# A row-sum of reciprocals: loads and chains of two rows in place of four, seven whole rows in place of sixteen, six single rows at the end

## The chip, the core and the metric

The kernel runs on one core of a Trainium2 chip; the other cores are idle. The time is the device time in microseconds of one execution. A single-core run is judged fast when it lies within 1.5% of the fastest of the same kernel.

The engines are named as the profile names them: DVE is VectorE, ACT is ScalarE, POOL is GpSimd, SP issues the loads.

## The reference

```python
x: (32, 512, 1024) float32, positive           # 67.1 MB
return np.sum(1.0 / x, axis=-1)                # 16384 sums
```

Each of the 128 partitions gets 128 rows of 1024 numbers. A "row" below always means one such row in each of the 128 partitions: 512 KB.

## The kernel before

A row is summed in one of two ways.

- By product ("chain"). For the two halves a and b of a row, 1/a + 1/b = (a + b) / (ab). POOL forms the products ab (512 numbers for 1024), ACT takes Ln and then Exp(-Ln) of them, which is 1/(ab), and DVE multiplies the row by it and sums. The work on ACT is halved, and POOL and DVE are brought in.
- Whole. ACT takes Ln and Exp(-Ln) of all 1024 numbers and sums in the same pass. POOL and DVE do nothing.

`GROUPS` lists (rows by product, whole rows, engine of the product), and each group is one load and one chain:

```python
    GROUPS = (
        [(1, 1, GP), (2, 0, GP)]
        + [(3, 1, GP), (4, 0, GP)] * 14
        + [(3, 1, GP), (2, 0, GP), (2, 0, GP)]
        + [(1, 0, GP), (1, 0, GP), (1, 0, GP), (1, 0, DV)]
    )
    xpool = ... bufs=8        # loaded rows: 8 x 4 rows x 4 KB per partition
    ppool = ... bufs=4        # products
    rpool = ... bufs=2, PSUM  # 1/(ab)
    # ... cut ...
    for np_, ns, eng in GROUPS:
        n = np_ + ns
        xt = xpool.tile([P, n, D], f32, tag="xt")
        nc.sync.dma_start(out=xt, in_=x_v[:, c0 : c0 + n, :])
        pr = ppool.tile([P, np_, H], f32, tag="pr")
        eng.tensor_tensor(out=pr, in0=xt[:, :np_, :H], in1=xt[:, :np_, H:], op=mult)
        for j in range(np_, n):
            # ... whole rows: ACT Ln, ACT Exp with accum_out ...
        nc.scalar.activation(out=pr, in_=pr, func=Ln, scale=S)
        rc = rpool.tile([P, np_, H], f32, tag="rc")
        nc.scalar.activation(out=rc, in_=pr, func=Exp, scale=-1.0)
        for j in range(np_):
            # ... DVE: row * rc, summed into sums[:, c0 + j] ...
        c0 += n
    nc.sync.dma_start(out=out_v, in_=sums)
```

The build schedules the instructions: within an engine their order need not be the order written.

Of the kernel before, what the change touches and what calls it, by code (L numbers as in the profile page):

```python
# [1 line left out]

# [5 lines left out]


@with_exitstack  # L10
def kernel(
    ctx: ExitStack,
    tc: tile.TileContext,
    x: bass.AP,
    out: bass.AP,
):







    nc = tc.nc
    f32 = mybir.dt.float32
    P = 128
    D = 1024
    H = D // 2
    F = 128

    S = float(2**17)


    GP, DV = nc.gpsimd, nc.vector
    GROUPS = (
        [(1, 1, GP), (2, 0, GP)]
        + [(3, 1, GP), (4, 0, GP)] * 14
        + [(3, 1, GP), (2, 0, GP), (2, 0, GP)]
        + [(1, 0, GP), (1, 0, GP), (1, 0, GP), (1, 0, DV)]
    )  # L40

    Ln = mybir.ActivationFunctionType.Ln
    Exp = mybir.ActivationFunctionType.Exp
    mult = mybir.AluOpType.mult
    add = mybir.AluOpType.add

    x_v = x.flatten_outer_dims().rearrange("(p f) d -> p f d", p=P)
    out_v = out.flatten().rearrange("(p f) -> p f", p=P)

    act_sets = list(get_activation_tables(nc.m.arch).keys())  # L50
    nc.scalar.add_instruction(  # L51
        mybir.InstLoadActFuncSet(
            name=nc.get_next_instruction_name(),
            act_func_set_id=act_sets.index("natural_log_exp_and_others"),
            ins=[],
            outs=[],
        )
    )

    xpool = ctx.enter_context(tc.tile_pool(name="xpool", bufs=8))  # L60
    ppool = ctx.enter_context(tc.tile_pool(name="ppool", bufs=4))
    opool = ctx.enter_context(tc.tile_pool(name="opool", bufs=1))
    rpool = ctx.enter_context(
        tc.tile_pool(name="rpool", bufs=2, space=bass.MemoryType.PSUM)
    )

    sums = opool.tile([P, F], f32)

    c0 = 0
# [7 lines that stand above are left out]
            nc.scalar.activation(out=xt[:, j, :], in_=xt[:, j, :], func=Ln)  # L77
            nc.scalar.activation(  # L78
                out=xt[:, j, :],
                in_=xt[:, j, :],  # L80
                func=Exp,
                scale=-1.0,
                accum_out=sums[:, c0 + j : c0 + j + 1],
# [5 lines that stand above are left out]
            row = xt[:, j, :].rearrange("p (h e) -> p h e", h=2)  # L89
            nc.vector.tensor_tensor_reduce(  # L90
                out=row,
                in0=row,
                in1=rc[:, j, :].unsqueeze(1).to_broadcast([P, 2, H]),
                scale=S,
                scalar=0.0,
                op0=mult,
                op1=add,
                accum_out=sums[:, c0 + j : c0 + j + 1],
            )
        c0 += n  # L100
    assert c0 == F, c0

    nc.sync.dma_start(out=out_v, in_=sums)


# [1 line left out]
_INS = ['x']  # L107
_OUTS = [((32, 512), 'float32')]


# [23 lines left out]
```

## Time and profile before

| | before |
|---|---|
| time, first three runs | 179.79 us (179.39 to 180.21) |
| span of the profiled run (itself 180.0 us) | 178.2 us |
| the stream in the middle | 425 to 432 GB/s, DMA share 1.00 to 1.01 |
| ACT, DVE, POOL in the middle | 90%, 84%, 82% |
| last load landed | 162.7 us |
| from last landing to the end ("lag" below) | 15.5 us |

The table of stages of the kernel before; the columns are the stretch, its length, the busy time of each engine with its instructions, the granted clock, the DMA share (the mean busy share of the 16 DMA engines) and the GB/s:

```profile
core 0: us, DVE busy (x) ACT busy (x) POOL busy (x), PEclk, DMA share, GB/s
20.00:40.00 20.00, 13.10 (x23) 14.55 (x12) 13.90 (x5) 1.00 1.01 426
60.00:80.00 20.00, 16.76 (x31) 17.92 (x17) 16.41 (x5) 1.00 1.00 425
100.00:120.00 20.00, 16.75 (x29) 17.91 (x15) 16.41 (x5) 1.00 1.01 432
...
160.00:165.00 5.00, 4.64 (x9) 4.77 (x6) 4.23 (x4) 1.00 0.19 79
165.00:170.00 5.00, 5.00 (x9) 2.96 (x5) 0.00 (x0) 1.00 0.00 0
```

Read it from two ends. In the middle the DMA engines are full and no compute engine is: the load stream sets the pace. After 162.7 us nothing is loaded any more, and from 165 us DVE alone is full. These are the two terms of the time: the stream, and what is still to be done when it ends.

The stream runs near the most that can be had. The Trainium skill gives the fabric's ceiling as 435 GB/s ("DMA: Bandwidth & Descriptors", Specifications); the 425 to 432 GB/s here are 98 to 99% of it.

The trace also records when each load lands, as one mark by each of 16 DMA engines. A load counts as landed at its last mark. (To set these records against the span I took POOL's first product to start 0.06 us after the first landing.) In the middle a 2 MB load lands every 4.89 us: 1.22 us per row.

POOL at the end, from the timeline of the kernel before; the columns are start, duration, engine, line, operation, and the idle time before it:

```profile
137.70 4.54 POOL L75 TENSOR_TENSOR pr<-xt 128x2048 f32<-128x2048 f32 x1 [1.46 <-DMA xt<-in_x_dram]
142.60 3.45 POOL L75 TENSOR_TENSOR pr<-xt 128x1536 f32<-128x1536 f32 x1 [0.36 <-DMA xt<-in_x_dram]
147.50 4.54 POOL L75 TENSOR_TENSOR pr<-xt 128x2048 f32<-128x2048 f32 x1 [1.45 <-DMA xt<-in_x_dram]
152.38 11.91 POOL L75 TENSOR_TENSOR pr<-xt 128x1536 f32<-128x1536 f32 x6 [0.35 <-DMA xt<-in_x_dram]
```

POOL waits for every load until 152.38, then does six products back to back. DVE's reductions, which stand 1.14 us apart when nothing holds them up, run without a gap from 161.03 to the last row's product, which its timeline shows:

```profile
172.45 0.68 DVE L75 TENSOR_TENSOR pr<-xt 128x512 f32<-128x512 f32 x1
```

(The chain of waits, next, counts it from 172.53, when the reduction before it is done.) The last row is DVE's own from the product on, and the chain of waits of the kernel before ends with it:

```profile
172.53 0.61 DVE pr L75
173.14 0.02 issue
173.16 0.64 ACT pr L85
173.80 0.02 issue
173.82 0.61 ACT rc L87
174.44 0.02 issue
174.46 1.22 DVE xt L90
```

Product, Ln, Exp and reduction of the last row, 3.2 us one after the other, and another 2.5 us for the store.

### The profile page before, as it was taken

Reading aid. Unit: us, or ns where it says so; the run is one execution under the profiler, and the core shown is the slowest. Engines: PE = TensorE matmul, PEld = TensorE weight load, DVE = VectorE, ACT = ScalarE, POOL = GpSimd, SP = SyncE. Lnnn points to the kernel's source line nnn. Section 1 sums busy time; section 2 is a strip of 40 time slices with the busy share of each in tenths; the row PEclk is TensorE's granted clock in tenths of the full one; section 3 lists DMA queues with packets and bytes.
Section 4 is the critical chain, followed back from the end, with each engine's and each line's share of the span. In section 5 each row is a group of like instructions: output and inputs, shape, how many; then the busy total and the mean of one; then the engine's idle time right before and its main releaser. Section 6 shows DMA issues by size and latency. Waiting matters only on the chain. (4 is left out here: it accounts for less than half of the span.)

```text
span 178.2 us, 617 instructions
## 1 busy us (share of the span) xinstructions
DVE 131.3 (74%) x225; ACT 142.9 (80%) x123; POOL 127.4 (71%) x40
## 2 busy tenths in 40 slices
DVE  0043629749697987979797979879797979799982
ACT  2757399396998979797979989797979799899531
POOL 0446946959789696969697896969696978998000
DMA  5999899999999999999999999999999999991000
GB/s 202 445 416 430 349 423 438 412 416 430 449 416 416 450 423 416 434 439 419 416 449 427 416 430 445 419 416 449 427 416 421 452 416 414 409 365 66 0 0 15
DMA packets 5477, 67.22 MB, mean 377 GB/s; under 512 B 608, under 2 KB 736, under 8 KB 1248
## 3 DMA queue, kind: packets, MB, share of 16 engines
q1 hardware_dynamic: 5472, 67.18, 89.8%
q14 instruction: 5, 0.04, 0.1%
HBM read 67.11 MB, written 0.07 MB: 377 GB/s over the span
## 5 line engine op out<-in xcount | busy, mean ns | idle before, releaser
L90 DVE CUSTOM_DVE_ANT_1 xt<-xt,rc 128x1024 f32<-128x1024 f32 x112 | 130.4, 1218 | 44.4 <-POOL pr L75 18.8
L75 POOL TENSOR_TENSOR pr<-xt 128x1536 f32<-128x1536 f32 (+3 forms) x36 | 127.2, 3540 | 36.6 <-DMA xt<-in_x_dram 36.6
L85 ACT ACTIVATE pr<-pr 128x1536 f32<-128x1536 f32 (+3 forms) x37 | 54.9, 1486 | 22.8 <-POOL pr L75 20.6
L87 ACT ACTIVATE rc<-pr 128x1536 f32<-128x1536 f32 (+3 forms) x37 | 54.3, 1467 | 3.6 <-DVE sums L90 2.6
L77 ACT ACTIVATE xt<-xt 128x1024 f32<-128x1024 f32 x16 | 16.7, 1042 | 3.9 <-DMA xt<-in_x_dram 3.9
L78 ACT ACTIVATE xt<-xt 128x1024 f32<-128x1024 f32 x16 | 16.9, 1057 | 0.5
L90 DVE DVE_READ_ACCUMULATOR2_ANT sums<- 128x1 f32 x112 | 9.2, 82 | 0.0
L78 ACT ACTIVATION_READ_ACCUMULATOR xt<-xt 128x1 f32 x16 | 3.0, 186 | 0.0
L51 ACT ACT_TABLE_LOAD x1 | 1.3, 1283 | 0.7 <-PEq L118 0.7
L75 DVE TENSOR_TENSOR pr<-xt 128x512 f32<-128x512 f32 x1 | 0.7, 684 | 0.0
L118 POOL MEMSET const-float32-0.0<- 128x1 f32 x1 | 0.1, 98 | 0.2 <-issue 0.2
L118 POOL MEMSET const-bfloat16-1.0<- 128x1 bf16 x1 | 0.1, 101 | 0.0
L118 POOL MEMSET const-uint8-127<- 128x1 uint8 x1 | 0.1, 101 | 0.0
L118 POOL MEMSET const-float32-1.0<- 128x1 f32 x1 | 0.1, 98 | 0.0
## 6 DMA issues: line engine op xcount, KB each, us to landing
xt<-in_x_dram SPq DMA_DIRECT2D x29, 2048.0 KB, 26.7
xt<-in_x_dram SPq DMA_DIRECT2D x4, 1024.0 KB, 14.6
xt<-in_x_dram SPq DMA_DIRECT2D x4, 512.0 KB, 12.8
out_dram<-sums SPq DMA_DIRECT2D x1, 64.0 KB, 1.5
```

Of the source, the lines that this page charges most:

```text
L51: nc.scalar.add_instruction(mybir.InstLoadActFuncSet(name=nc.get_next_instruction_name(), act_func_set_id=act_sets.index("natural_log_exp_ ...
L75: eng.tensor_tensor(out=pr, in0=xt[:, :np_, :H], in1=xt[:, :np_, H:], op=mult)
L77: nc.scalar.activation(out=xt[:, j, :], in_=xt[:, j, :], func=Ln)
L78: nc.scalar.activation(out=xt[:, j, :], in_=xt[:, j, :], func=Exp, scale=-1.0, accum_out=sums[:, c0 + j : c0 + j + 1],)
L85: nc.scalar.activation(out=pr, in_=pr, func=Ln, scale=S)
L87: nc.scalar.activation(out=rc, in_=pr, func=Exp, scale=-1.0)
L90: nc.vector.tensor_tensor_reduce(out=row, in0=row, in1=rc[:, j, :].unsqueeze(1).to_broadcast([P, 2, H]), scale=S, scalar=0.0, op0=mult, op ...
L118: nc = _bacc.Bacc("TRN2", target_bir_lowering=False, num_devices=1)
```

## The change

Its intent: loads and chains of two rows let each engine start sooner and leave less behind when the stream ends; fewer whole rows relieve ACT, the busiest compute engine. The buffered bytes stay the same.

```diff
     GROUPS = (
-        [(1, 1, GP), (2, 0, GP)]
-        + [(3, 1, GP), (4, 0, GP)] * 14
-        + [(3, 1, GP), (2, 0, GP), (2, 0, GP)]
-        + [(1, 0, GP), (1, 0, GP), (1, 0, GP), (1, 0, DV)]
+        ([(2, 0, GP)] * 4 + [(1, 1, GP)] + [(2, 0, GP)] * 3) * 7
+        + [(2, 0, GP)] * 5
+        + [(1, 0, GP)] * 4 + [(1, 0, GP), (1, 0, DV)]
     )
...
-    xpool = ctx.enter_context(tc.tile_pool(name="xpool", bufs=8))
+    xpool = ctx.enter_context(tc.tile_pool(name="xpool", bufs=16))
```

## The prediction

> **What bounds the kernel now.** The load stream. The table of stages shows a DMA share of 1.00 to 1.01 and 425 to 432 GB/s in every 20 us stage from 20 to 140 us. The Trainium skill ("DMA: Bandwidth & Descriptors", Specifications) gives 435 GB/s as the fabric ceiling, so this is about 98% of it and cannot be sped up. In the same stages ACT is 90% busy, DVE 84%, POOL 82%: none is full, and the groups table puts all of POOL's 36.6 us of waiting on loads. Successive 2 MB landings in the trace are 4.89 us apart, 1.22 us per row.
>
> The second term is the tail. Loads stop at about 162 us, the span is 178.2. The timeline shows POOL working six products back to back until 164.3, then VectorE alone reducing its backlog of ten rows gaplessly at 1.14 us each until 172.5, then the last row's serial chain (0.68 + 0.63 + 0.60 + 1.22 us) and the store. The chain of waits contains only this end.
>
> **What changes.** All loads shrink from 2 MB to 1 MB (67 loads instead of 37); buffered bytes are unchanged (16 x 2 rows for 8 x 4), so the queue should stay full. Nine rows move from ScalarE alone to the three-engine path.
>
> *Loads, cost.* Packets become 8 KB: the packet records show 611 to 615 ns for 16 KB, 309 to 314 for 8 KB, 159 for 4 KB, i.e. some 9 ns fixed per packet. The same page ("Why small descriptors are slow") names a fixed cost per packet; the trace agrees. Two rows should take 2.47 to 2.495 us (seen between 1 MB landings at start and end), against 2.446. Over some 58 pairs: +1.3 to +2.8 us, plus about 0.1 for two more single-row loads. All on the critical path.
>
> *Engines, per 16 rows (now 19.8 us of loads).* POOL: 7 x 2.37 + 1.28 = 17.9 us. ACT: 7 x 2.07 + 1.22 + 2.15 = 17.9. DVE: 15 x 1.14 = 17.1. All below 19.8, so the middle stays bound by loads, with POOL's margin per pair only about 0.1 us. Fewer whole rows therefore buy nothing.
>
> *Tail, gain.* The lag behind the loads shrinks. Now the last three-row and two-row groups leave VectorE ten rows behind when POOL ends. After: the last pair lands some 7.5 us before the last load; then POOL 2.4, ACT 2.1, VectorE 2.3 + 5 single rows x 1.14, product to reduction 3.2, store 2.5. This is bound by VectorE: the end falls about 10.6 us after the last landing instead of about 15.4: some 4.5 us won.
>
> Net: about -2 to -3 us of 179.8. A small recurrence over these measured durations, which reproduces the span before to 0.2 us, gives 174.8 to 177.3 us of span.
>
> **Predicted: 177.2 us (175.3 to 179.2).** Faster by over 2%: 0.26; within 2%: 0.70; slower: 0.04.
>
> **What would show each step.** Loads: 8 KB packets at 309 to 314 ns; landings of pairs about 2.48 us apart; loads ending 1.5 to 3 us later, near 164. Middle: DMA share still 1.00, POOL about 90% busy and still waiting on loads. Tail: VectorE reduces gaplessly to the last row, but its last product begins near 169 to 170 instead of 172.5.
>
> **What would make it wrong.** POOL's 0.1 us margin vanishes (more waits per group), making the middle POOL-bound and the tail longer. DMA stalls: one near 16 to 19 us holds some engines about 2 us now; another count of these moves the result by as much. Two-deep PSUM with two-row tiles could stall ScalarE behind VectorE. If 8 KB packets cost nothing extra in a long stream, the gain exceeds 2%.

The "small recurrence" named there goes through the groups in order. A product starts when its load has landed and POOL is free; Ln when the product is done and ACT is free; Exp also waits until one of the two PSUM tiles is free; the reductions start when Exp is done and DVE is free. Every duration is one read from the trace before. The experiments' expectations use it too.

## The result, and the profile after

| | before | after |
|---|---|---|
| median time | 179.63 us (4 runs, 179.39 to 180.21) | 177.09 us (4 runs, 176.94 to 177.36) |
| ratio | | 0.9856, 95% interval 0.9828 to 0.9883 |
| span of the profiled run | 178.2 us | 174.9 us |
| landings, middle | 4.89 us per four rows | 2.485 us per two rows |
| last load landed | 162.7 us | 163.9 us |
| lag from there to the end | 15.5 us | 11.1 us |

A ratio is the mean time of one kernel's fast runs over that of the other's of the same rounds, so it is not quite the ratio of the medians. The change gains 1.4%, within the 2% that count here as the same. The two profiles differ by 3.3 us and the medians by only 2.5: about 0.4 us of that is the profiled run of before, one of its slower ones (180.0 us), and 0.3 us lies outside the spans (the time exceeds the span by 1.8 us before and by 2.1 after).

The table of stages of the changed kernel:

```profile
20.00:40.00 20.00, 19.18 (x33) 18.27 (x21) 17.92 (x9) 1.00 1.01 422
60.00:80.00 20.00, 17.92 (x31) 17.63 (x20) 17.89 (x9) 1.00 1.02 423
100.00:120.00 20.00, 16.97 (x31) 16.68 (x19) 16.94 (x9) 1.00 1.01 420
...
160.00:165.00 5.00, 4.87 (x9) 4.09 (x7) 4.89 (x4) 1.00 0.40 158
165.00:170.00 5.00, 4.70 (x9) 2.79 (x6) 0.00 (x0) 1.00 0.00 0
```

The DMA engines are still full, but move 420 to 424 GB/s in place of 425 to 432. POOL and DVE are 85 to 90% busy in these stretches from 60 us on, instead of 82% and 84%. The stream still ends near the same time (158 GB/s in the stretch from 160 to 165), and now less is left to do. Two lines of the changed kernel's DVE timeline, and then the end of its chain of waits:

```profile
167.87 1.22 DVE L89 CUSTOM_DVE_ANT_1 xt<-xt,rc 128x1024 f32<-128x1024 f32 x1
169.01 0.69 DVE L74 TENSOR_TENSOR pr<-xt 128x512 f32<-128x512 f32 x1
```

```profile
169.09 0.62 DVE pr L74
...
169.73 0.64 ACT pr L84
...
170.39 0.61 ACT rc L86
...
171.02 1.22 DVE xt L89
```

The last row's product begins at 169.01 in place of 172.45, straight after the reduction before it; DVE has no gap from 161.01 on. The last row's serial chain is as long as it was.

One thing was not as supposed. SP's own waits, of the kernel before and then of the changed kernel (total us, times, longest):

```profile
SPq L73 <- DVE sums L90: 137.5, 29, 7.6
```

```profile
SPq L72 <- DMA xt<-in_x_dram: 123.1, 59, 3.1
```

and the pages' lists of issues, with the KB of one and the median us to landing, in the same order:

```profile
xt<-in_x_dram SPq DMA_DIRECT2D x29, 2048.0 KB, 26.7
```

```profile
xt<-in_x_dram SPq DMA_DIRECT2D x61, 1024.0 KB, 19.8
```

Before, SP waits for DVE to free a buffer. After, it waits for earlier loads to land, and a load lands 19.8 us after it was issued: eight periods of 2.485 us. So eight loads are in flight, not the 12 or 13 that 16 buffers would leave room for (a pair is in work for 7.1 us from its landing to its last reduction, three periods). In both traces the loads carry eight different semaphores (counters that a landing raises and that an engine can wait on), taken in turn, and the issuing instructions of the changed kernel's trace show what holds the others back. The first eight loads are issued from 0.74 to 4.50 us without a wait. From the ninth on, the program itself makes SP wait for the semaphore of the load eight before: the first load lands at 5.54 and the ninth is issued at 5.55, the second at 8.35 and the tenth at 8.36. The limit is thus the built program's own; these runs show none of the chip's.

### The profile page after: what moved, and what is told of

Read it like the earlier page. It is cut to its first block, busy times and chain, and to the rows that moved or that the text cites. A ratio compares the mean times of both kernels' runs of the same rounds, so it can differ in the third digit from the quotient of the medians.

```text
span 174.9 us, 826 instructions
## 1 busy us (share of the span) xinstructions
DVE 143.5 (82%) x243; ACT 141.0 (81%) x156; POOL 142.7 (82%) x70
## 5 line engine op out<-in xcount | busy, mean ns | idle before, releaser
L89 DVE CUSTOM_DVE_ANT_1 xt<-xt,rc 128x1024 f32<-128x1024 f32 x121 | 142.5, 1219 | 28.7 <-ACT rc L86 14.2
L74 POOL TENSOR_TENSOR pr<-xt 128x1024 f32<-128x1024 f32 (+1 forms) x66 | 142.5, 2164 | 21.9 <-DMA xt<-in_x_dram 14.8
L84 ACT ACTIVATE pr<-pr 128x1024 f32<-128x1024 f32 (+1 forms) x67 | 64.8, 969 | 25.7 <-POOL pr L74 23.5
L86 ACT ACTIVATE rc<-pr 128x1024 f32<-128x1024 f32 (+1 forms) x67 | 63.1, 942 | 3.5 <-DVE sums L89 1.8
L89 DVE DVE_READ_ACCUMULATOR2_ANT sums<- 128x1 f32 x121 | 10.0, 83 | 0.0
L76 ACT ACTIVATE xt<-xt 128x1024 f32<-128x1024 f32 x7 | 7.3, 1040 | 0.0
L77 ACT ACTIVATE xt<-xt 128x1024 f32<-128x1024 f32 x7 | 7.3, 1040 | 0.0
L77 ACT ACTIVATION_READ_ACCUMULATOR xt<-xt 128x1 f32 x7 | 1.3, 186 | 0.0
## 6 DMA issues: line engine op xcount, KB each, us to landing
xt<-in_x_dram SPq DMA_DIRECT2D x61, 1024.0 KB, 19.8
```

What stands on the lines that cost most here:

```text
L76: nc.scalar.activation(out=xt[:, j, :], in_=xt[:, j, :], func=Ln)
L77: nc.scalar.activation(out=xt[:, j, :], in_=xt[:, j, :], func=Exp, scale=-1.0, accum_out=sums[:, c0 + j : c0 + j + 1],)
L89: nc.vector.tensor_tensor_reduce(out=row, in0=row, in1=rc[:, j, :].unsqueeze(1).to_broadcast([P, 2, H]), scale=S, scalar=0.0, op0=mult, op ...
```

## The experiments

The theory: (1) the middle is bound by the stream, so the mix of rows does not matter; (2) smaller packets make the stream about 2 us longer; (3) the finer end shortens the lag by about 4.5 us. The rivals: chains of two in the middle, or fewer whole rows, are what gains; or the sizes of the last few groups alone gain it and could have been had without the dearer stream.

The experiments use a loop in which one load may feed several chains. `p` is a pair by product, `w` one row by product and one whole, `s` a single row by product, `d` the same with its product on DVE, `S` a single whole row. Each inner list is one load. Written so, the changed kernel is

```python
([[p]]*4 + [[w]] + [[p]]*3) * 7 + [[p]]*5 + [[s]]*5 + [[d]]
```

All twelve gave correct results. "Landed" and "lag" are of the profiled run of each. The changed kernel was not run in these calls: comparisons with it go by the medians or the ratios of different calls, and the median of the kernel before went from 179.35 to 179.93 over the calls. e5, the changed kernel but for its buffers, shows how well it repeats.

| run | time, us | before | ratio (95%) | landed | lag |
|---|---|---|---|---|---|
| e1 fine middle, old end | 181.67 | 179.40 | 1.0125 (1.0111 to 1.0139) | 163.5 | 15.9 |
| e2 old middle, fine end, first try | 179.42 | 179.40 | 1.0004 (0.9991 to 1.0018) | 166.0 | 11.6 |
| e3 2 MB loads, fine chains, first try | 178.38 | 179.40 | 0.9942 (0.9930 to 0.9955) | 164.7 | 11.7 |
| e4 last row whole on ACT | 174.64 | 179.40 | 0.9735 (0.9722 to 0.9748) | 163.9 | 8.6 |
| e5 8 buffers | 177.09 | 179.36 | 0.9872 (0.9856 to 0.9889) | 163.9 | 11.1 |
| e6 14 whole rows | 176.72 | 179.36 | 0.9854 (0.9839 to 0.9868) | 164.0 | 11.1 |
| e7 old chains, 1 MB loads | 181.54 | 179.36 | 1.0121 (1.0106 to 1.0136) | 163.9 | 15.9 |
| e8 2 MB loads, fine end, first try | 175.20 | 179.36 | 0.9771 (0.9756 to 0.9785) | 162.1 | 11.3 |
| e9 e2 mended | 179.59 | 179.35 | 1.0013 (0.9994 to 1.0032) | 162.3 | 15.7 |
| e10 e3 mended | 176.43 | 179.35 | 0.9832 (0.9817 to 0.9847) | 161.7 | 12.4 |
| e11 e8 mended | 173.20 | 179.35 | 0.9657 (0.9642 to 0.9671) | 161.9 | 9.1 |
| e12 old middle for 60 rows only | 176.19 | 179.93 | 0.9789 (0.9760 to 0.9819) | 163.4 | 11.0 |

### What the stream costs: e7

```diff
-        nc.sync.dma_start(out=xt, in_=x_v[:, c0 : c0 + n, :])
+        for k in range(0, rows, 2):     # the kernel before, each tile by loads of two rows
+            m = min(2, rows - k)
+            nc.sync.dma_start(out=xw[:, k : k + m, :], in_=x_v[:, c0 + k : c0 + k + m, :])
```

> The kernel before with one thing changed: each four-row tile is loaded by two DMAs of two rows. Chains, buffers and ending as before. Theory (8 KB packets cost 1.5% per byte): loads end about 2.2 us later, lag at the end unchanged, 181 to 182.5 us. Rival (the number and size of loads costs nothing; fine chains cost or gain everything): 179.6 us.

It took 181.54 us, 2.2 us more than the kernel before, with nothing changed but the size of loads. Its page's lists of issues and its DMA line, beside which the page of before has 26.7 us for 29 loads of 2 MB and 89.8%:

```profile
q1 hardware_dynamic: 9648, 67.18, 90.1%
...
xw<-in_x_dram SPq DMA_DIRECT2D x62, 1024.0 KB, 19.9
```

The extra time is in the packets. A load of two rows is cut into packets of 8 KB, of four into 16 KB. The records give a median of 312 ns for 8 KB (changed kernel) and of 613 for 16 KB (kernel before): twice the small one is about 1.8% more. As a share, 90.1% of e7's span of 179.8 us against 89.8% of 178.2 is 2.0 us more of packet time. The Trainium skill names a fixed cost of about three cycles per packet ("DMA: Bandwidth & Descriptors", Why small descriptors are slow); 2 x 312 - 613 = 11 ns for the extra packet here is a cost of that kind, but no run separates that mechanism from others. That fewer bytes are in flight is not the reason: e5 below has on average 5.1 loads in flight from 20 to 140 us, the changed kernel 8.0, at the same time and the same 2.485 us per pair. The size of the cost is measured, by the times. (In e7's own profile the last landing is only 1.2 us after that of before, 163.9 against 162.7, because in the profile of before some DMA engines had lost time, which is told below. By the marks of the fastest engine the stream from first to last landing took 156.7 us against 154.4, 2.3 us more.) (2) holds.

### The two halves of the change: e1 and e5, e6

e1 joins the new middle to the old end:

```diff
-        + [[p]]*5 + [[s]]*5 + [[d]]
+        + [[(4, 0, GP)], [(3, 1, GP)], [p], [p]] + [[s]]*3 + [[d]]
```

> The first 112 rows as in the changed kernel (1 MB loads, chains of two), the last 16 as in the kernel before (a four, a three with a whole row, two pairs, four singles). Theory (the change is a dearer load stream plus a shorter lag at the end): loads end about 2 us later than in the kernel before, the lag from last landing to end is the old 15 to 16 us, so the time is above that of the kernel before, by 0.5 to 2.5 us: 180 to 182 us. Rival 1 (chains of two in the middle are themselves what saves time): about 177 us, as the changed kernel.

(e1 has 14 buffers of two rows and 2 of four.) 181.67 us, 1.25% slower than before, with the old lag: 15.9 us. Its DVE timeline shows how the chain of four makes the lag. DVE, in step with the pairs until then, stands idle for 6.38 us before the first reduction of that chain:

```profile
157.23 1.22 DVE L101 CUSTOM_DVE_ANT_1 xw<-xw,rc 128x1024 f32<-128x1024 f32 x1 [6.38 <-POOL pr L83]
```

The rival that chains of two in the middle gain by themselves falls: without the fine end there is only the dearer stream. Between e1 and the changed kernel lie 0.0269 of the time before, 4.8 us, and they lie in the end.

e6 doubles the whole rows, e5 halves the buffers:

```diff
-    ([[p]]*4 + [[w]] + [[p]]*3) * 7
+    ([[p]]*2 + [[w]] + [[p]]*3 + [[w]] + [[p]]) * 7          # e6
-    xpool ... bufs=16
+    xpool ... bufs=8                                         # e5
```

> The changed kernel with 14 whole rows in place of 7 (two groups of one and one in each cycle of eight); POOL's share in the middle falls from 90 to about 85%. Theory (the middle is bound by loads, so the mix does not matter): same as the changed kernel within 0.4 us, 176.7 to 177.5. Rival (POOL, nearly full, sets the pace): 0.5 us or more faster. Rival (ScalarE sets it): slower by over 0.5 us.

> The changed kernel with 8 load buffers of two rows in place of 16. The changed kernel's queue waited on landings, not on freed buffers, and a load took 19.8 us from issue to landing, which is eight periods of 2.49 us. If eight loads in flight is a limit other than the buffers, 16 buffers buy little: with 8, four or five loads stay in flight beside three or four in work, the DMA share stays 1.00 and the time is within 0.5 us of the changed kernel, 176.6 to 177.6. Rival (the depth of 16 keeps the stream full): loads fall behind, over 178 us.

e5 took 177.09 us, to the hundredth the median of the changed kernel: 16 buffers buy nothing here. With eight of them SP waits for DVE's releases again, and the stream stays full. What holds 16 buffers to eight loads in flight is the program's own wait, told above; this run shows that the depth does not matter here.

e6 took 176.72 us. That is 0.2% under e5, with intervals that overlap, and the landing and the lag are the same within 0.1 us. From 60 to 140 us POOL is busy 83% of the time in place of 88% in the changed kernel, and ACT 92% in place of 87%. Neither shows in the time beyond that 0.2%, so neither set the pace: (1) holds. Of the 0.37 us between the two medians only 0.1 us is left in the spans of the same runs (174.8 to 175.1 against 175.0 to 175.1); the rest lies outside them.

### What the last row costs: e4

```diff
-        + [[s]]*5 + [[d]]
+        + [[s]]*5 + [[S]]
```

> The changed kernel with its last row given to ScalarE whole (two activations of 1024, about 2.15 us) in place of the chain product, Ln, Exp, reduction behind VectorE's queue (3.2 us). If the end is bound by VectorE's backlog followed by that serial chain, ScalarE's row runs beside VectorE's last reductions and the end falls by about 2.2 us: span about 172.7, 174.9 us. Rival (the end is bound by the last landing): no more than about 1 us less, 3.2 against 2.15.

174.64 us against the expected 174.9. The last row no longer queues behind DVE: in e4's timeline ACT's two activations run beside DVE's last reduction.

```profile
167.52 1.04 ACT L86 ACTIVATE xw<-xw 128x1024 f32<-128x1024 f32 x1
167.87 1.22 DVE L100 CUSTOM_DVE_ANT_1 xw<-xw,rc 128x1024 f32<-128x1024 f32 x1
168.59 1.06 ACT L87 ACTIVATE xw<-xw 128x1024 f32<-128x1024 f32 x1
169.77 0.35 SPq L114 DMA_DIRECT2D out_dram<-sums  x1
```

The last landing did not bound the end; DVE's queue and the serial chain after it did. The rival allowed at most 1 us; 2.5 us came by the medians, 2.2 by the ratios.

### Can the fine end be had without the dearer stream: e2, e3, e8, first tries

e2 keeps the old middle and makes only the last 20 rows fine, e3 feeds two chains of the new middle from one 2 MB load, e8 joins this to a better end:

```python
[[w], [p]] + [[(3, 1, GP)], [(4, 0, GP)]]*13 + [[p]]*7 + [[s]]*5 + [[d]]             # e2
[[p, p], [p, p], [w, p], [p, p]]*7 + [[p]]*5 + [[s]]*5 + [[d]]                       # e3
([[p, p], [p, p], [w, p], [p, p]]*7)[:26] + [[p]]*11 + [[s], [S]]                    # e8
```

all three with 8 buffers of four rows, as before.

> The middle as before (2 MB loads, chains of four), only the last 20 rows as in the changed kernel: seven pairs, six singles. Theory 1 in its simple form (the tail is set by the sizes of the last groups): loads end as before, the lag shrinks by 4.5 us, so 175 us. Theory 2 (POOL leaves the last chain of four about 2 us behind the loads and gains only about 0.13 us on them per pair, 2.36 against 2.49, so seven pairs do not let it catch up): a recurrence over the measured durations gives a gain of only 1 us: 178.5 to 179 us, the lag from last landing to end still about 15 us.

> Chains in order and size as in the changed kernel, but the first 112 rows are loaded four rows at a time (2 MB, 16 KB packets). Loads should end 2 us sooner than in the changed kernel if the packets cost what their records say. Theory 2 (POOL's lag behind the loads survives to the end): the last 2 MB load leaves POOL one pair behind, about 2 us, of which five pairs recover some 0.6; the lag at the end is about 12.4 us in place of 10.7 to 11, and the time only 0.3 to 0.8 us below the changed kernel: 176.3 to 176.8. Rival (lag set by the last groups only): 175 us. Rival (packet size costs nothing in a long stream): 177 us or more, with loads ending no sooner.

> A version built from both theories: 26 loads of 2 MB with chains of two, then eleven loads of a pair, so that POOL can catch up (11 times 0.13 us), then one single row and the last row whole on ScalarE. Loads should end 1.7 us sooner than in the changed kernel and the lag from last landing to end should be about 9 us: span 171.1, 173 us, faster than both kernels, by 2.3% and 3.7%. If POOL's lag is not recovered as supposed, 174 to 175.

e2's time came 0.4 us above what its theory 2 expected, and not for the reason expected: its stream ended at 166.0, not at 162. e3 and e8 missed by about 2 us each. The profiles show two flaws of the experiments. The first is in e2's page, in the 35th to 37th of the 40 slices of its GB/s:

```profile
GB/s 194 448 421 439 435 376 424 439 428 428 421 439 426 428 421 439 424 430 417 443 428 424 421 439 428 424 428 432 432 421 410 422 421 421 361 239 226 27 0 15
```

361, 239, 226: the stream was starved. A single row takes a whole four-row buffer, eight buffers hold few rows, and so the last loads of e2 and of e3 waited for DVE and landed up to 2.6 us apart instead of 1.24.

The second is in e8's timeline, as in e3's; Ln is line 95, Exp line 97:

```profile
137.16 1.06 ACT L95 ACTIVATE pr<-pr 128x1024 f32<-128x1024 f32 x1 [0.96 <-POOL pr L82]
137.76 1.22 DVE L100 CUSTOM_DVE_ANT_1 xw<-xw,rc 128x1024 f32<-128x1024 f32 x1
138.12 1.98 ACT L97 ACTIVATE rc<-pr 128x1024 f32<-128x1024 f32 x2
```

Two Exp in a row: when one load feeds two chains, the build orders ACT as Ln, Ln, Exp, Exp. The first chain's Exp then waits behind the second chain's Ln, which waits for POOL (0.96 us in the first line); the two chains act like one of four rows.

### The same again, mended: e10, e9, e11

Small loads got 11 buffers of their own and four-row loads 5 (room for 42 rows in place of 32), and each activation was tied to follow the one written before it, with no wait added:

```diff
+    x4pool = ... bufs=5
-    xpool = ... bufs=8
+    xpool = ... bufs=11
-        nc.scalar.activation(...)
+        with tc.issue_after(last[0].ins):
+            last[0] = nc.scalar.activation(...)
```

> 2 MB loads for the first 112 rows with chains of two, with the same two flaws removed (own buffers for small loads; Ln, Exp, Ln, Exp held in the order written). Theory: loads end about 2 us sooner than in the changed kernel, the lag grows from about 11 to 12.4 us because POOL is one pair behind after the last big load: span 174.5, 176.4 us. Rival (the first try's loss of 1.3 us against the changed kernel came from the big loads themselves): 178 us again.

> The old middle with the fine tail again, without two flaws of the first try: there eight buffers ran out at the end (single rows took whole slots and the last loads landed 2.1 to 2.6 us apart in place of 1.24), and the build had put two Ln of ScalarE ahead of two Exp. Here the small loads have 11 buffers of their own, the four-row ones 5, and the activations are held in the order written. Simple form (only the last groups' sizes count): loads end as in the kernel before, the lag is 11 us, 174 us of span. POOL-lag form (POOL is still more than 1 us behind after seven pairs, VectorE then has the singles queued): lag 15 us, 177.7 us of span, 179.4 us. If it lies between, the buffers were what cost the first try.

> 26 loads of 2 MB with chains of two, eleven pairs, a single row and the last row whole on ScalarE, with the two flaws removed. Theory: loads end near 162, lag about 9 us, span 171.1, 173 us: 3.6% under the kernel before. If order and buffers were not what the first try (175.2 us) lost by, it stays at 175.

All three came within 0.2 us of the times of their theories (of e9's two forms, that of the POOL lag). e10 ends its stream 2.2 us sooner than the changed kernel and loses 1.3 us of it again in the lag: 176.43 us. That fits what e7 measured from the other side. e11 is faster than both kernels: 173.20 us, 3.4% under the kernel before and 2.0% (by the ratios) to 2.2% (by the medians) under the change. In e8 the stream had ended on time, at 162.1, so the 2 us between e8 and e11 are in the lag (11.3 against 9.1). I put them down to the order of ACT's instructions. Buffers and order were changed together, but the two traces part them: each of the 39 loads lands in e8 at most 0.3 us after the same load in e11, and the load buffers can act on the engines only through the landings, so at least 1.7 of the 2 us are the order's. A run with the order alone was not made. In e3 against e10 it was the buffers that cost the end: the loads are at most 0.4 us apart up to the last two, which land 1.7 and 3.0 us later in e3.

e9 is the telling one. The last 20 rows were as fine as in the changed kernel, the stream ended at 162.3, and nothing was gained: a lag of 15.7 us, 179.59 us. The expectation blamed POOL. The timeline of e9 blames DVE; its first two reductions of the last chain of four, and its last two:

```profile
145.94 1.22 DVE L112 CUSTOM_DVE_ANT_1 xw<-xw,rc 128x1024 f32<-128x1024 f32 x1 [2.23 <-issue]
147.09 1.22 DVE L112 CUSTOM_DVE_ANT_1 xw<-xw,rc 128x1024 f32<-128x1024 f32 x1
...
171.06 1.22 DVE L112 CUSTOM_DVE_ANT_1 xw<-xw,rc 128x1024 f32<-128x1024 f32 x1
172.20 0.69 DVE L94 TENSOR_TENSOR pr<-xw 128x512 f32<-128x512 f32 x1
```

From 145.94 to 172.20 DVE never pauses: 4 + 14 + 5 = 23 rows at 1.142 us are 26.3 us. The last chain of four lands at 137.3, and its first reduction can only start 8.6 us later, after a four-row product, Ln and Exp. POOL too works without a gap from 137.42 to 160.67, but from 145.94 on DVE never waits for it, and at the end POOL is idle at times (its waits of up to 1.0 us there are for ACT). A pair costs DVE 2.28 us and the stream 2.49, so DVE gains 0.2 us per pair; seven pairs give back 1.4 us.

### How long the lag lasts: e12

If so, some 5 us of lag at 0.2 us per pair take some 25 pairs, and the fine chains must begin that far before the end. e12 has 31:

```diff
-    [[w], [p]] + [[(3, 1, GP)], [(4, 0, GP)]]*13 + [[p]]*7  + [[s]]*5 + [[d]]
+    [[w], [p]] + [[(3, 1, GP)], [(4, 0, GP)]]*7  + [[p]]*31 + [[s]]*5 + [[d]]
```

> The same as the old middle with the fine tail, but the chains of two begin earlier: 60 rows in groups of four as before, then 31 pairs and six singles, own buffers for the small loads, activations in the order written. In the version with only seven pairs VectorE, not POOL as its expectation had it, reduced gaplessly from the last chain of four to the end: it gains only 2.49 - 2.28 = 0.2 us per pair. Theory (a lag of some 5 us is worked off at 0.2 us per pair, so about 25 pairs are needed): the lag from last landing to end falls from 15 to about 10.7 us, span 173.9, 175.8 us, 1.3 us under the changed kernel. VectorE should have gaps again before the end. Rival (chains of four anywhere before the fine tail keep the lag): 179.4 us as with seven pairs.

176.19 us, where 175.8 was expected; the lag is 11.0 us, that of the changed kernel. And DVE has caught up before the end. e12's timeline shows the first reduction of the last chain of four at 86.70, from there on reductions starting in steps of 1.14 until 149.50, and then gaps again. These are 56 reductions: the four rows and 26 pairs, where the sum said about 25.

```profile
148.36 1.22 DVE L112 CUSTOM_DVE_ANT_1 xw<-xw,rc 128x1024 f32<-128x1024 f32 x1
149.50 1.22 DVE L112 CUSTOM_DVE_ANT_1 xw<-xw,rc 128x1024 f32<-128x1024 f32 x1
...
154.28 1.22 DVE L112 CUSTOM_DVE_ANT_1 xw<-xw,rc 128x1024 f32<-128x1024 f32 x1
155.62 1.22 DVE L112 CUSTOM_DVE_ANT_1 xw<-xw,rc 128x1024 f32<-128x1024 f32 x1
```

The rival, that chains of four anywhere ahead keep the lag, falls. The expectation's further point, 1.3 us under the changed kernel, came out as 0.9 us by the medians, 1.2 by the ratios; its stream ended 0.4 us sooner than the changed kernel's.

## Why the prediction was right

177.2 us was predicted and 177.09 measured. That the two agree to 0.1 us is partly luck: the recurrence gave a span of 174.8 to 177.3, and the measured 174.9 lies at its lower edge, while the time outside the span was 2.1 us in place of before's 1.8. Point by point:

- *The stream gets dearer by 1.4 to 2.9 us.* Right. e7 measured 2.2 us for the small loads alone. In the profile of the changed kernel the last landing came only 1.2 us later, less than predicted, because a chance effect hid some of it (its size differs from run to run): before, the 16 marks of the last load were spread over 3.1 us, since some DMA engines had stood still for up to 2 us on the way; after, over 1.9 us. By the fastest engine's marks the stream from first to last landing grew from 154.4 to 156.8 us, 2.4 us.
- *Pairs land 2.48 us apart, packets of 8 KB take 309 to 314 ns.* Right: 2.485 us, and a median of 312 ns.
- *The middle stays bound by loads; fewer whole rows buy nothing.* Right: DMA share 1.01 to 1.02, and e6, with 14 of them, took the same within 0.2%. POOL's narrow margin held: it went on waiting for loads.
- *The lag falls from 15.4 to 10.6 us, and the last product starts near 169 to 170.* Right: 15.5 to 11.1, and 169.01. The end was bound by DVE, as said, and e4 showed that the last landing did not bound it.
- *The buffered bytes are unchanged, so the queue should stay full.* The queue did stay full, but not through the buffers: the program's own waits allow only eight loads in flight, and 8 buffers did as well as 16 (e5).
- *The gain of the tail comes from the small groups at the end.* The prediction set the last three-row and two-row groups of before against the last pairs of after. That is only half of it. e9 has the same last pairs and gains nothing. The number came right all the same, because the recurrence goes through every group and not only the last (for e2, the same groups as e9, it gave a gain of only 1 us); the reason written beside it would have promised e9 the gain. The lag is made by the last chain of four and is worked off at 0.2 us per pair, so what gains is that the last chain of four, if there is one, lies far enough back: 7 pairs were too few (e9), 31 enough (e12), where DVE had caught up after 26.

So the expected gain of a 4.5 us shorter lag was there (4.4 in the profiles); about half of it was paid back to the stream.

## What to carry to other kernels

When, as here, a stream sets the pace and the other engines are 80 to 90% busy, look at how far the slowest engine lags behind the stream: that set the end. A long chain makes that lag, and it shrank only by the difference of the two periods per group, here 0.2 us of 2.49, so shorten the chains well ahead of the end and keep the loads large: 2 MB loads that each feed two chains, eleven loads of a pair, a single row and a last row on an engine that is free beat both kernels (173.2 us). Look at the order in which the build issues each engine's work, and at the buffers that small tiles take, before you believe an experiment: mending them gave back 2 us in e3 and 2 us in e8, and the first times had looked like results.

## What the Trainium skill lacked or had wrong

- "DMA: Bandwidth & Descriptors", Where 436 GB/s comes from: it says that for HBM to SBUF transfers the HBM side, about 358 GB/s, binds, and does not say at that place that this needs both cores of a pair streaming (its section Measured does). With the other cores idle this one loaded 425 to 432 GB/s for over 100 us. "HBM Reference", Specifications (TRN2), has it right: a core alone measures about 425.
- "DMA: Bandwidth & Descriptors", Measured: its table gives the time of a DMA by its size, with nothing between 1 and 16 MB, and its rule of at least 1 MiB per DMA gives no price for 1 MB against 2 MB in a full queue. Here it is 1.6%: 2 x 2.485 us against 4.89, and 2.2 us of 179 (e7).
- No page that I read says that a built program may keep only eight loads in flight. Here 16 buffers of two rows gave eight (19.8 us from issue to landing at 2.485 us each): the program takes eight semaphores in turn and has SP wait for the landing of the load eight before. Whether the chip has a limit of its own no run shows.
- No page that I read has what a DMA engine's standstill does on this load path: in the trace before some engines lost about 2 us near 20 us, the spread of a load's 16 marks jumped from 0.33 to 2.25 us, and it was 3.1 us at the end, so none of it was made up there.
